# Own memory for the output projection's split activations, squares summed by VectorE, one tile for mean and deviation

## The chip, the cores and the metric

The kernel runs on one core of a Trainium2 chip. The metric is the device time of one execution in microseconds, the median over the runs shown. The profile is one further execution, recorded instruction by instruction.

## The reference

One layer of a hybrid encoder on 512 positions with 2048 channels. A combined projection feeds four groups of 1024 channels and a gate of 4096; each group's result is normalised, gated and projected back.

```python
h = rms_norm(x, pre_g)
proj = h @ w_in
a, f, hy, q, gate = split(proj, [2G, 3G, 6G, 7G])
# group 0, Conformer
u = a_val * sigmoid(a_gate)              # a_val, a_gate: the halves of a
u = depthwise_conv(u, conv_dw_w, conv_dw_b)
u = silu(layer_norm(u, conv_ln_g, conv_ln_b))
y_a = u @ conv_pw_w + conv_pw_b
# group 1: Fourier mixing of f; group 2: Hyena long convolution of hy;
# group 3: attention of q into 256 memory tokens
y = rms_norm(concat([y_a, y_b, y_c, y_m]) per group, group_g)
y = y * silu(gate)
out = y @ w_out
return x + rms_norm(out, post_g)
```

The layer norm subtracts the mean over 1024 channels, takes the mean of the squares of what is left, and scales. The norm of a group takes the mean of squares of its 1024 channels.

## The kernel before

Channels lie on the 128 partitions, positions along the free dimension: a group is CT = 8 tiles of 128 x 512. A product in full precision is made of three matmuls of a 32-bit format that TensorE takes in one pass (`mm3`, L102 to L105): each operand is split by `split` (L77) into a high part, copied by ScalarE (L79), and a rest, subtracted by VectorE (L80). Weights come through three buffers each of `raw`, `wh` and `wl`, 128 x 1024 (`load`, `wload`). TensorE's results go to PSUM: six banks with the tag `pg`, two with the tag `pf`.

`gate(g, ct, ...)` (L624) projects one gate tile in 48 matmuls into a `pf` bank (`project`, L304), takes its Silu on ScalarE and multiplies it into tile ct of group g; the group's scale `rsg[g]` (`group_scale`, L489) is multiplied in at the same place, or later by `group_norm` (L493) for the tiles gated before the norm was known. `project` calls its argument `fill` after every 12 matmuls, so that a generator's steps are laid between them. `channel_rstd` (L478) makes the deviation from a tile of summed squares: eight column sums on TensorE (L149), root on ScalarE and reciprocal on VectorE (L134, L135), a diagonal matrix by VectorE and its product with ones on TensorE (`spread`, L143, L144), and a copy to the tile asked for (L145).

The part in question comes after the attention (group 3, pool `wp3`). A pool `wp5` is opened with `lnt` (four tiles of 128 x 512: mean, deviation and two for squares), `uH` and `uL`. The eight tiles of the convolution lose their mean (L927); their squares are summed into `vacc` by `group_square` (L471): ScalarE squares into one of the two `lnt` tiles, GpSimd adds (L476). Then come `gate(3, 4)` and the last three gates of group 3, with the steps of `layer_norm` (L931) between their matmuls: `channel_rstd(rstd, vacc)` after 36 matmuls of `gate(3, 5)`, then one channel tile per step. The pointwise product (L948 to L961) follows in two halves of four `pg` banks; its results are squared and summed into `gacc` in the same way. `gA` takes the memory of `uL` for seven gate tiles that were computed early and are loaded back (L964). `gate(0, 7)` is the last projection. `group_norm(0)` scales one tile, and the loop at L970 scales seven and multiplies in `gA`: 15 VectorE instructions. Then `wp5` closes.

The output projection opens the pool `wp4` in the memory that `wp5` had. It goes through rounds of 512 output columns. In each, 32 tiles n of `y` are split into `jh` and `jl` (three buffers each, L1034 to L1036), in the order of the groups 2, 1, 3, 0; each n is 12 matmuls (four blocks of positions, three products). A pair of n shares one `wh`, `wl`. The last 512 columns are done in two rounds of two blocks each, six matmuls per n, and the results are finished (`finish`, L986) and stored.

The order on each engine is set by a planner when the program is built. It plays the program through on a clock of its own and gives each engine, among the instructions that are ready there, the earliest in the program. A tile waits for a free buffer of its tag; a pool's tiles wait until every pool that had their memory before has been read to the end. On the chip each engine goes through its list in order.

Of the kernel before, what the change touches and what calls it, by code (L numbers as in the profile page):

```python
# [12 lines left out]
F32R = mybir.dt.float32r  # L13
I32 = mybir.dt.int32
AF = mybir.ActivationFunctionType
# [5 lines left out]
P = 128  # L21
# [21 lines left out]
def encoder_kernel(ctx: ExitStack, tc: tile.TileContext, a: dict, out: bass.AP):  # L43
    nc = tc.nc
    act, dve, pool, pe, sp = nc.scalar, nc.vector, nc.gpsimd, nc.tensor, nc.sync
    mul, add, sub = ALU.mult, ALU.add, ALU.subtract
# [16 lines left out]
    def nm(s):  # L63
        uid[0] += 1
        return f"{s}_{uid[0]}"
# [4 lines left out]
    def pg():  # L70
        return psg.tile([P, 512], F32, tag="pg", name=nm("pg"))

    def ytile(i, dt=F32):
        return yp.tile([P, 4, 512], dt, tag=f"y{i}", name=nm(f"y{i}"))
# [10 lines left out]
    def load(src, n=1024):  # L85
        raw = stg.tile([P, 1024], F32, tag="raw", name=nm("raw"))
        sp.dma_start(raw[:, :n], src)
        return raw
# [4 lines left out]
    def wsplit(src, n=512):  # L93
        h, l = wparts()
        split(h[:, :n], l[:, :n], src)
        return h[:, :n], l[:, :n]

    def wload(src):

        return wsplit(load(src), 1024)  # L100

    def mm3(ps, wh, wl, xh, xl, start, stop):  # L102
        pe.matmul(ps, wh, xh, start=start, stop=False)  # L103
        pe.matmul(ps, wh, xl, start=False, stop=False)  # L104
        pe.matmul(ps, wl, xh, start=False, stop=stop)  # L105
# [49 lines left out]
    wp = w0.enter_context(tc.tile_pool(name="wx", bufs=2))  # L155

    def wt(tag, shape=(P, 512), dt=F32, bufs=2):
        return wp.tile(list(shape), dt, tag=tag, name=nm(tag), bufs=bufs)
# [213 lines left out]
    wp = w0.enter_context(tc.tile_pool(name="wpn", bufs=2))  # L372
# [7 lines left out]
    wp = w0.enter_context(tc.tile_pool(name="wp0", bufs=2))  # L380
# [90 lines left out]
    def group_square(src, acc, sqt, first):  # L471
        if first:
            act.activation(acc, src, AF.Square)
        else:
            act.activation(sqt, src, AF.Square)
            pool.tensor_tensor(acc, sqt, acc, op=add)  # L476
# [56 lines left out]
    wp = w1.enter_context(tc.tile_pool(name="wp1", bufs=2))  # L533
# [73 lines left out]
    gacc = cst.tile([P, 512], F32, tag="gacc", name="gaccC", bufs=2)  # L607
    for ct in range(CT):
# [5 lines left out]
        y = yC[ct // 4][:, ct % 4, :]  # L614
# [9 lines left out]
    def gate(g, ct, tiles, fill=None):  # L624
        ps = project(48 + CT * g + ct, fill)
        sg = sgtile()
        act.activation(sg, ps, AF.Silu)
        y = tiles[ct // 4][:, ct % 4, :]
        if g in rsg:
            group_scale(g, ct, tiles)  # L630
        else:
            gated.append((g, ct))
        dve.tensor_tensor(y, y, sg, op=mul)
# [3 lines left out]
    wp = w2.enter_context(tc.tile_pool(name="wp2", bufs=1))  # L637
# [6 lines left out]
    wp = w2i.enter_context(tc.tile_pool(name="wp2a", bufs=2))  # L644
# [8 lines left out]
    for k in range(KD):  # L653
# [8 lines left out]
        jh = wt("jh", (P, 514), F32R)  # L662
        jl = wt("jl", (P, 514), F32R)
# [30 lines left out]
    wp = w2i.enter_context(tc.tile_pool(name="wp2b", bufs=2))  # L694
# [70 lines left out]
    gacc = cst.tile([P, 512], F32, tag="gacc", name="gaccB", bufs=2)  # L765
# [50 lines left out]
    wp = w3.enter_context(tc.tile_pool(name="wp3", bufs=2))  # L816
    gacc = cst.tile([P, 512], F32, tag="gacc", name="gaccM", bufs=2)
# [93 lines left out]
    w3.close()  # L911


    w5 = ctx.enter_context(ExitStack())
    wp = w5.enter_context(tc.tile_pool(name="wp5", bufs=1))
    lnt = wt("lnt", (P, 4, 512), bufs=1)
    uH = wt("uH", (P, CT, 512), F32R, 1)
    uL = wt("uL", (P, CT, 512), F32R, 1)
    mean = lnt[:, 0, :]
    rstd = lnt[:, 1, :]  # L920
    pm = pg()
    pe.matmul(pm, ones, csum, start=True, stop=True)
    act.activation(mean, pm, AF.Copy, scale=1.0 / G)
    vacc = cst.tile([P, 512], F32, tag="gacc", name="vacc", bufs=2)
    for ct in range(CT):
        y = acch[ct // 4][:, ct % 4, :]
        dve.tensor_tensor(y, y, mean, op=sub)  # L927
        group_square(y, vacc, lnt[:, 2 + ct % 2, :], ct == 0)
    gate(3, 4, yM)

    def layer_norm():  # L931
# [15 lines left out]
    gacc = cst.tile([P, 512], F32, tag="gacc", name="gaccA", bufs=2)  # L947
    for hf in range(2):  # L948
        accs = [pg() for _ in range(4)]
        for kp in range(4):  # L950
            wh, wl = wload(a["pw"][hf, kp])
            for kk in range(2):
                k = 2 * kp + kk
                for m in range(4):
                    s = slice(512 * kk + P * m, 512 * kk + P * m + P)
                    mm3(accs[m], wh[:, s], wl[:, s], uH[:, k, :], uL[:, k, :], k == 0, k == CT - 1)
        for m in range(4):
            y = yA[hf][:, m, :]
            ct = 4 * hf + m
            act.activation(y, accs[m], AF.Identity, bias=pw_b[:, ct:ct + 1])  # L960
            group_square(y, gacc, lnt[:, 2 + ct % 2, :], ct == 0)  # L961
    gA = wt("uL", (P, CT, 512), F32, 1)
    for ct in range(EARLY):
        sp.dma_start(gA[:, ct, :], gdm[:, ct, :])  # L964
# [5 lines left out]
    for ct in range(EARLY):  # L970
        group_scale(0, ct, yA)
        y = yA[ct // 4][:, ct % 4, :]
# [6 lines left out]
    wp = w4.enter_context(tc.tile_pool(name="wp4", bufs=3))  # L979
# [6 lines left out]
    def finish(m):  # L986
        t = cst.tile([P, 1], F32, tag="st", name=nm("st"), bufs=2)
        dve.tensor_reduce(t, ssq[:, m, :], axis=AX.X, op=add)
        rst = rstd_of(t, 1, 1.0 / D)
        act.activation(og[:, m, 3, :], og[:, m, 3, :], AF.Copy, scale=rst)  # L990
        pool.tensor_tensor(xres[:, m, 3, :], xres[:, m, 3, :], og[:, m, 3, :], op=add)
        for r in range(3):
            dve.scalar_tensor_tensor(xres[:, m, r, :], og[:, m, r, :], rst, xres[:, m, r, :], op0=mul, op1=add)
            if r == 1:
                sp.dma_start(out[P * m:P * m + P, 0:1024], xres[:, m, 0:2, :].rearrange("p a b -> p (a b)"))
        for r in (2, 3):
            sp.dma_start(out[P * m:P * m + P, 512 * r:512 * r + 512], xres[:, m, r, :])
# [5 lines left out]
    for r, ms in rounds:  # L1003
        held = []
        accs = {m: (pg if r % 2 == 0 or m < 2 else pf)() for m in ms}
        gb = wt("gb", bufs=2)
        sp.dma_start(gb, a["post_g"][512 * r:512 * r + 512].partition_broadcast(P))
        c0, c1 = P * ms[0], P * ms[-1] + P
        for kp in range(16):
            if ms[0] == 2 and kp in (3, 6):  # L1010
                finish(kp // 3 - 1)
            i = 2 * kp - 32 + LAST
            if ms[0] == 2 and i >= 0:
                if i == 0:
                    lw = [ytile(0, F32R), ytile(1, F32R), ytile(4), ytile(5)]
                raw = lw[2 + i // 4][:, i % 4:i % 4 + 2, :].rearrange("p a b -> p (a b)")
                sp.dma_start(raw, a["wo"][r, order[2 * kp] // 2])
            else:
                raw = load(a["wo"][r, order[2 * kp] // 2])
            if not (ms[0] == 2 and i >= 0):  # L1020
                wh2, wl2 = wsplit(raw, 1024)
            for kk in range(2):
                k = order[2 * kp + kk]
                n = 2 * kp + kk
                if ms[0] == 2 and n >= 32 - LAST:
                    w = raw[:, 512 * kk:512 * kk + 512]
                    wh, wl = lw[(i + kk) // 4][:, (i + kk) % 4, :], wt("lwl", dt=F32R, bufs=LAST)
                    split(wh, wl, w)
                    jh, jl = (wt(t, (P, 256), F32R, LAST) for t in ("ljh", "ljl"))
                    split(jh, jl, ys[k // CT][k % CT // 4][:, k % 4, c0:c1])  # L1030
                    held.append((n, jh, jl, wh, wl))
                    continue
                wh, wl = wh2[:, 512 * kk:512 * kk + 512], wl2[:, 512 * kk:512 * kk + 512]
                jh = wt("jh", dt=F32R, bufs=3)  # L1034
                jl = wt("jl", dt=F32R, bufs=3)
                split(jh[:, c0:c1], jl[:, c0:c1], ys[k // CT][k % CT // 4][:, k % 4, c0:c1])  # L1036
                for m in ms:
                    s = slice(P * m, P * m + P)
                    mm3(accs[m], jh[:, s], jl[:, s], wh, wl, n == 0, n == 31)
        for m in ms:  # L1040
            for n, jh, jl, wh, wl in held:
                s = slice(P * m - c0, P * m - c0 + P)
                mm3(accs[m], jh[:, s], jl[:, s], wh, wl, False, n == 31)
            act.activation(og[:, m, r, :], accs[m], AF.Square, accum_out=ssq[:, m, r:r + 1])
            dve.tensor_tensor(og[:, m, r, :], accs[m], gb, op=mul)
            if ms[0] == 2:
                finish(m)
        if r == 2:
            act.activation(warm, ssq[:, 0, 2:3], AF.Sqrt)
# [119 lines left out]
```

## Time and profile before

| | us |
|---|---|
| runs (three) | 1730.17, 1731.67, 1737.29 |
| median | 1731.67 |
| the profiled execution | 1736.26 |
| its span in the profile | 1734.0 |

| engine | busy us | share of the span |
|---|---|---|
| TensorE (PE), matmuls | 1687.0 | 97% |
| TensorE, weight loads (PEld) | 1424.7 | 82% |
| VectorE (DVE) | 1205.5 | 70% |
| ScalarE (ACT) | 752.3 | 43% |
| GpSimd (POOL) | 151.4 | 9% |

Times in the rows are microseconds from the start of the span; the second number of a timeline row is how long the instructions of that row took together. A bracket at the end of a row is the engine's idle time before it and what ended that. Neighbouring matmuls overlap in the trace: a matmul's row says 0.39 us where the next starts after 0.23. PEclk is TensorE's granted clock as a share of its higher level.

### The profile page before, as it was taken

The numbers are of one execution on the slowest core, as the hardware profiler recorded it, in microseconds if no ns is written. First come the engines' busy times: TensorE is split into PE (matmuls) and PEld (weight loads), VectorE is DVE, ScalarE is ACT, GpSimd is POOL, SyncE is SP. The second block draws the span as 40 slices with busy tenths as digits, with TensorE's granted clock in tenths as the row PEclk, the third lists the DMA queues.
The fourth block names the chain that finished last, engine by engine and source line by source line (L and its number), as shares of the span: only waits on it lengthen the run. The fifth ranks groups of instructions, "written<-read, shape, count | busy, mean of one in ns | idle before, by whom it ended". The sixth has DMA issues, their size and how long they took to land.

```text
span 1734.0 us, 22272 instructions
## 1 busy us (share of the span) xinstructions
PE 1687.0 (97%) x8521; PEld 1424.7 (82%) x8521; DVE 1205.5 (70%) x1755; ACT 752.3 (43%) x1121; POOL 151.4 (9%) x98
## 2 busy tenths in 40 slices
PE   7999999999999999999999999999999699999997
PEld 5987888888888888888888898888878588888876
DVE  7966988478587686878765879986462545454586
ACT  6645655232223222223434346445453444444564
POOL 4201432000000000000000011100021100000000
PEclk9999999999999999999999999999999899999999
DMA  8654443432222322223333234232222523232355
GB/s 285 226 186 150 158 146 134 158 95 88 98 93 90 97 98 91 77 82 116 128 116 128 94 117 158 98 109 86 74 85 97 200 98 104 98 103 98 117 206 182
DMA packets 80575, 215.13 MB, mean 124 GB/s; under 512 B 8146, under 2 KB 25810, under 8 KB 79956
## 3 DMA queue, kind: packets, MB, share of 16 engines
q1 hardware_dynamic: 80468, 213.70, 36.5%
q8 instruction: 67, 1.10, 0.3%
q14 instruction: 40, 0.33, 0.1%
HBM read 195.05 MB, written 18.63 MB: 123 GB/s over the span
## 4 chain that ended last, share of the span: by engine, by line
PE 87%; DVE 7%; issue 2%; ACT 2%; DMA 2%; POOL 1%; SPq 0%; DVEq 0%; ACTq 0%; POOLq 0%
PE pf L105 16%; PE pf L103 16%; PE pf L104 16%; PE pg L103 12%; PE pg L104 12%; PE pg L105 12%; DVE y L516 2%; DVE wl L80 2%; DMA raw<-in_wv_dram 1%; POOL vacc L476 1%; ACT wh L79 1%; DMA kdm<-mst 0%; PE pg L558 0%; DVE y L491 0%; PE pg L411 0%
## 5 line engine op out<-in xcount | busy, mean ns | idle before, releaser
L103 PE MATMUL pf<-hH,wh 128*128 128x512 f32 x1280 | 504.7, 394 | 0.0
L105 PE MATMUL pf<-hH,wl 128*128 128x512 f32 x1280 | 502.1, 392 | 0.0
L104 PE MATMUL pf<-hL,wh 128*128 128x512 f32 x1280 | 501.5, 392 | 0.0
L80 DVE TENSOR_TENSOR wl<-raw,wh 128x1024 fp32r<-128x1024 f32 (+1 forms) x288 | 359.1, 1249 | 187.0 <-ACT wh L79 185.8
L79 ACT ACTIVATE wh<-raw 128x1024 fp32r<-128x1024 f32 (+1 forms) x288 | 298.3, 1037 | 358.9 <-PE pf L104 275.8
L103 PEld LDWEIGHTS pf<-hH,wh 128*128 128x128 f32 x1280 | 241.8, 189 | 47.7 <-issue 0.8
L105 PEld LDWEIGHTS pf<-hH,wl 128*128 128x128 f32 x1280 | 241.5, 189 | 47.4 <-issue 0.5
L104 PEld LDWEIGHTS pf<-hL,wh 128*128 128x128 f32 x1280 | 241.4, 189 | 47.2 <-issue 0.2
L80 DVE TENSOR_TENSOR jl<-y,jh 128x512 fp32r<-128x512 f32 (+1 forms) x154 | 91.5, 597 | 121.2 <-ACT jh L79 120.1
L79 ACT ACTIVATE jh<-y 128x512 fp32r<-128x512 f32 (+1 forms) x154 | 84.5, 550 | 179.3 <-PE pg L104 113.0
L103 PE MATMUL pg<-wh,jh 128*128 128x512 f32 x384 | 150.5, 392 | 11.2 <-ACT jh L79 11.2
L104 PE MATMUL pg<-wl,jh 128*128 128x512 f32 x384 | 150.2, 391 | 0.0
L105 PE MATMUL pg<-wh,jl 128*128 128x512 f32 x384 | 150.1, 391 | 0.0
L103 PEld LDWEIGHTS pg<-wh,jh 128*128 128x128 f32 x384 | 72.6, 189 | 26.4 <-ACT jh L79 11.5
L516 DVE SCALAR_TENSOR_TENSOR y<-ubuf,par,y 128x512 f32<-128x512 f32 x120 | 89.8, 748 | 2.5
L105 PEld LDWEIGHTS pg<-wh,jl 128*128 128x128 f32 x384 | 72.5, 189 | 15.4 <-DVE jl L80 0.2
L104 PEld LDWEIGHTS pg<-wl,jh 128*128 128x128 f32 x384 | 72.7, 189 | 15.1
L79 ACT ACTIVATE uH<-pp 128x512 fp32r<-128x512 f32 x16 | 10.1, 632 | 92.9 <-DVE pp L585 92.9
L516 DVE SCALAR_TENSOR_TENSOR y<-ub,par,y 128x512 f32<-128x512 f32 x60 | 46.4, 773 | 2.3 <-ACT y L514 1.1
L427 POOL TENSOR_TENSOR y<-fsq,y 128x512 f32<-128x512 f32 x24 | 43.6, 1815 | 41.5 <-ACT fsq L426 41.4
L104 PE MATMUL pf<-wl,jh 128*128 128x512 f32 x116 | 45.2, 390 | 1.3 <-DVE wl L80 1.3
L516 DVE SCALAR_TENSOR_TENSOR y<-ubm,par,y 128x512 f32<-128x512 f32 x60 | 45.2, 753 | 0.8
(374 smaller groups left out, 2847.3 us busy)
## 6 DMA issues: line engine op xcount, KB each, us to landing
raw<-in_w_std_dram SPq DMA_DIRECT2D x160, 512.0 KB, 3.8
raw<-in_wo_dram SPq DMA_DIRECT2D x77, 512.0 KB, 3.3
raw<-in_wk_dram SPq DMA_DIRECT2D x16, 512.0 KB, 4.0
kd<-y SPq DMA_DIRECT2D x16, 512.0 KB, 3.5
y<-kd SPq DMA_DIRECT2D x32, 256.0 KB, 3.3
raw<-in_w_f_dram SPq DMA_DIRECT2D x16, 512.0 KB, 3.3
raw<-in_wv_dram SPq DMA_DIRECT2D x15, 512.0 KB, 5.9
y<-in_xT_dram SPq DMA_DIRECT2D x8, 512.0 KB, 6.8
```

Source lines behind the costliest of these rows:

```text
L79: act.activation(h, src, AF.Copy)
L80: dve.tensor_tensor(l, src, h, op=sub)
L103: pe.matmul(ps, wh, xh, start=start, stop=False)
L104: pe.matmul(ps, wh, xl, start=False, stop=False)
L105: pe.matmul(ps, wl, xh, start=False, stop=stop)
L427: pool.tensor_tensor(acc, sq, acc, op=add)
L476: pool.tensor_tensor(acc, sqt, acc, op=add)
L516: dve.scalar_tensor_tensor(o, u[:, t:t + L], conv_w[:, ct, t:t + 1], o, op0=mul, op1=add)
```

## The change

It opens a small pool `wj` ahead of `wp5`, below it in memory, and keeps it open to the end. In round 0 all `jh` and `jl` come from `wj`, two buffers each; in later rounds two of three n take theirs from `wj` and the third from one buffer in `wp4`. `lnt` goes; one tile, `stat`, holds first the mean and then the deviation. The squares of the layer norm go to PSUM banks (`pg`) and are added by VectorE instead of GpSimd; those of group 0 go through the `stat` tile and are added by VectorE.

```diff
+    wj = ctx.enter_context(tc.tile_pool(name="wj", bufs=2))
     w5 = ctx.enter_context(ExitStack())
     wp = w5.enter_context(tc.tile_pool(name="wp5", bufs=1))
-    lnt = wt("lnt", (P, 4, 512), bufs=1)
     uH = wt("uH", (P, CT, 512), F32R, 1)
     uL = wt("uL", (P, CT, 512), F32R, 1)
-    mean = lnt[:, 0, :]
-    rstd = lnt[:, 1, :]
+    mean = rstd = wt("stat", bufs=1)
...
         dve.tensor_tensor(y, y, mean, op=sub)
-        group_square(y, vacc, lnt[:, 2 + ct % 2, :], ct == 0)
+        sq = vacc if ct == 0 else pg()
+        act.activation(sq, y, AF.Square)
+        if ct:
+            dve.tensor_tensor(vacc, sq, vacc, op=add)
...
             act.activation(y, accs[m], AF.Identity, bias=pw_b[:, ct:ct + 1])
-            group_square(y, gacc, lnt[:, 2 + ct % 2, :], ct == 0)
+            sq = gacc if ct == 0 else rstd
+            act.activation(sq, y, AF.Square)
+            if ct:
+                dve.tensor_tensor(gacc, sq, gacc, op=add)
...
-                jh = wt("jh", dt=F32R, bufs=3)
-                jl = wt("jl", dt=F32R, bufs=3)
+                jp, nb = (wj, 2) if r == 0 or n % 3 else (wp, 1)
+                jh, jl = (jp.tile([P, 512], F32R, tag=t, name=nm(t), bufs=nb) for t in ("jh", "jl"))
```

## Rows read from the trace of the kernel before

**Rows 1.** The page: busy time of each engine, share of the span, instructions.

```profile
PE 1687.0 (97%) x8521; PEld 1424.7 (82%) x8521; DVE 1205.5 (70%) x1755; ACT 752.3 (43%) x1121; POOL 151.4 (9%) x98
```

**Rows 2.** Stretches: length, busy PE, PEld, DVE, ACT, POOL; PEclk, DMA share, GB/s.

```profile
1251.50:1267.20 15.70, 15.70 (x71) 12.83 (x70) 13.20 (x15) 6.58 (x11) 10.14 (x5) 1.00 0.10 34
1267.20:1278.70 11.50, 7.99 (x29) 6.59 (x29) 6.46 (x10) 6.23 (x8) 3.05 (x3) 0.70 0.27 91
1300.60:1355.00 54.40, 54.40 (x242) 45.04 (x241) 13.99 (x11) 23.96 (x35) 10.82 (x7) 1.00 0.36 121
1355.00:1372.00 17.00, 2.93 (x18) 2.36 (x16) 12.77 (x23) 4.38 (x7) 0.00 (x0) 0.63 0.76 308
```

**Rows 3.** TensorE's timeline at the layer norm: start, duration, line, operands, idle before.

```profile
1251.47 0.47 PE L103 MATMUL pf<-hH,wh 128*128 128x512 f32 x1
...
1267.01 0.39 PE L105 MATMUL pf<-hH,wl 128*128 128x512 f32 x1
1270.91 1.87 PE L149 MATMUL pg<-ones,vacc 128*128 128x1 f32 x8 [3.51 <-POOL vacc L476]
```

**Rows 4.** TensorE's timeline at the entry of the output projection.

```profile
1354.99 0.95 PE L149 MATMUL pg<-ones,gaccA 128*128 128x1 f32 x8
...
1371.94 0.80 PE L103 MATMUL pg<-wh,jh 128*128 128x512 f32 x1 [11.19 <-ACT jh L79]
...
1376.89 0.40 PE L103 MATMUL pg<-wh,jh 128*128 128x512 f32 x1
```

**Rows 5.** The chain of work that ended last, in order of time: start, us, what.

```profile
1249.97 0.44 PE pg L144 x4
...
1274.27 0.43 PE pf L103
...
1361.42 2.08 DVE y L491 x3
...
1370.45 0.70 DVE y L973
```

**Rows 6.** Timelines of GpSimd and VectorE around both places.

```profile
1237.72 1.30 POOL L476 TENSOR_TENSOR gaccM<-sq,gaccM 128x512 f32<-128x512 f32 x1 [36.09 <-ACT sq L475]
1256.75 12.31 POOL L476 TENSOR_TENSOR vacc<-lnt,vacc 128x512 f32<-128x512 f32 x6 [15.70 <-ACT lnt L475]
...
1255.26 4.30 DVE L927 TENSOR_TENSOR y<-y,lnt 128x512 f32<-128x512 f32 x7
1259.48 1.78 DVE L491 SCALAR_TENSOR_TENSOR y<-y,par,rsg 128x512 f32<-128x512 f32 x1
1261.18 2.31 DVE L80 TENSOR_TENSOR wl<-raw,wh 128x1024 fp32r<-128x1024 f32 x1
...
1356.04 1.22 DVE L80 TENSOR_TENSOR wl<-raw,wh 128x1024 fp32r<-128x1024 f32 x1 [1.43 <-ACT wh L79]
```

**Rows 7.** ScalarE's and VectorE's groups from 1200 us on: busy us, mean ns, idle.

```profile
L79 ACT ACTIVATE wh<-raw 128x1024 fp32r<-128x1024 f32 x100 | 104.8, 1049 | 51.6 <-PE pf L104 26.1 <-PE pg L104 23.1 <-issue 1.8
L79 ACT ACTIVATE jh<-y 128x512 fp32r<-128x512 f32 x96 | 60.4, 631 | 154.8 <-PE pg L104 96.1 <-PE pf L104 48.8 <-DVE y L973 9.9
L1044 ACT ACTIVATE og<-pg 128x512 f32<-128x512 f32 x12 | 7.1, 595 | 1.5 <-PE pg L105 1.5
...
L80 DVE TENSOR_TENSOR wl<-raw,wh 128x1024 fp32r<-128x1024 f32 x100 | 124.6, 1246 | 88.2 <-ACT wh L79 88.0
L80 DVE TENSOR_TENSOR jl<-y,jh 128x512 fp32r<-128x512 f32 x96 | 66.4, 693 | 115.5 <-ACT jh L79 114.4 <-PE pg L104 1.1
L1045 DVE TENSOR_TENSOR og<-pg,gb 128x512 f32<-128x512 f32 x12 | 8.1, 689 | 1.4 <-ACT og L1044 1.3
```

**Rows 8.** TensorE's timeline in the last round.

```profile
1688.66 0.50 PE L104 MATMUL pf<-wl,jh 128*128 128x512 f32 x1 [1.28 <-DVE wl L80]
```

**Rows 9.** SP's queue of loads at the entry of the output projection.

```profile
1371.21 0.80 SPq L1007 DMA_DIRECT2D gb<-in_post_g_dram  x2
1382.47 11.21 SPq L87 DMA_DIRECT2D raw<-in_wo_dram  x3
```

## The prediction

> **What bounds the kernel now.** I read the page's busy times first: TensorE has 97% of the span [rows 1]. So a change is worth what it takes out of TensorE's gaps, and the table by stretches, from the last attention head on, tells where they are: 1267.2 to 1278.7 has TensorE at 7.99 of 11.50 us with a granted clock of 0.70, and 1355 to 1372 has it at 2.93 of 17.00 [rows 2]. TensorE's timeline names what it waits for there: 3.51 us for GpSimd's `vacc`, 11.19 us for ScalarE's `jh` [rows 3, 4]. The change touches these two places; call them A (layer norm) and B (entry of the output projection).
>
> **A, as it is.** The 69 matmuls from 1251.47 to 1267.01 come every 0.228 us [rows 3]: the last 33 of gate (3,4) and 36 of gate (3,5). Then TensorE idles, does its eight column sums in 1.87 us, where the same eight take 0.95 in B [rows 3, 4], and ten matmuls come every 0.43 us [rows 5]: behind the idle time the clock is at the lower of its levels (1.2 GHz), then back at 2.4. The work from 1267.24 to 1278.81, twelve matmuls further, is 0.95 + 2 x 0.44 (eight spread matmuls [rows 5]) + 12 x 0.228 = 4.6 us. The rest, 11.6 - 4.6 = **7.0 us**, is loss.
>
> **A, changed.** Removed: seven GpSimd adds, of which six stand in a chain of 12.31 us, 2.05 each; one with VectorE idle takes 1.30 [rows 6]. VectorE's work among them is stretched too: a scale of L491 takes 1.78 us (0.68 alone, as in the chain of B, three in 2.08 [rows 5]), a `wl` 2.31 (1.25) [rows 6, 7]. Added: seven VectorE adds of a PSUM and an SBUF operand. The nearest row is L1045, 0.689 us, as long as the SBUF pair of `jl`, 0.693 [rows 7]; seven subtractions in a row take 4.30, so 0.61 each [rows 6]. ScalarE's squares now write PSUM, which no row shows. A ScalarE copy within SBUF takes 0.631, a square out of PSUM 0.595 [rows 7]: 0.04 either way, 0.3 us for seven. I take zero, since they lie beside VectorE's work. (The Trainium skill, Trace Analysis, Optimizing Scalar/DVE Operations, gives VectorE some 65 ns more for an access to PSUM than to SBUF; by that seven adds would be 0.5 us longer, while the rows of L1045 and `jl` show no difference.)
>
> VectorE's queue decides what is left. Every engine goes in order, in an order fixed by the planner: of what its own clock has ready, the earliest in the program. From 1252.0 on VectorE has 8 subtractions and 7 adds at 0.61, five scales at 0.68, and then `wl` for the second half of gate (3,5) at 1.25: 9.2 + 3.4 + 1.25 = 13.8, done at 1265.8. TensorE wants it for that half's third matmul, 33 + 24 + 2 after 1251.47: 1264.9. So a stall of up to 0.9 us, none if a hole lets `wl` forward; I take 0.6. The sum in `vacc` is then ready near 1265, before TensorE comes to its place at 1267.2. A stall of 1.28 us elsewhere left the clock alone [rows 8]. **A gives 7.0 - 0.6 = 6.4 us**; bounds 2.6 (rival 4) and 7.0.
>
> **B, as it is.** Gate (0,7) ends, column sums to 1355.94, root on ScalarE, spread, then 15 multiplications of group 0 on VectorE from 1361.42 to 1371.15, then `jh`, then the first matmul of round 0 at 1371.94 [rows 4, 5]. That `jh` reads group 2, finished long before. It waits for memory: its pool opens only when all of `wp5`, `gA` with it, has been read, and the load of `gb`, which depends on no result, starts at 1371.21 as well [rows 9]. Round 0's first matmuls are at the low clock again; the 13th starts at 1376.89 [rows 4].
>
> **B, changed.** `wj` lies below `wp5`, where `wp3` was until about 1241. Two pairs `jh`, `jl` can be split in holes long before: ScalarE is busy 23.96 and VectorE 13.99 of 54.4 us from 1300.6 [rows 2]. Cost zero; 2 x (0.63 + 0.69) without holes. The weights of round 0's first three pairs of k are split by 1357.3 even now [rows 6]. So round 0 starts behind the column sums, at 1355.94, while the norm's chain goes on. 24 matmuls for two `jh` and the spread are 5.5 + 0.9, to 1362.3. The third `jh` gets its buffer after 12 matmuls, at 1358.7, and its `jl`, 0.63 + 0.69 later, comes before the multiplications. The fourth gets its buffer at 1362.3, and its `jl` is late: VectorE has begun the 15, which stand earlier in the program and block it to 1371.15. TensorE does n = 2 (to 1365.0) and the 8 of 12 matmuls of n = 3 that need no `jl` (to 1366.8), and idles 5.1 us until `jl` at 1371.9: long enough for the low clock, so ten more at 0.43, to 1376.4. At 1376.89 it has 44 + 10 + 2 = 56 matmuls behind it instead of 12: 44 x 0.228 = **10.0 us**. The planner's clock may shift one `jl` either way (rivals 1, 2).
>
> **The other pieces.** Adds of group 0's squares: seven at 0.69 on a VectorE that has 40 us of holes there. With one scratch tile each square waits for the add before it, and on ScalarE the next evictions and a `wh`, wanted two pairs later, stand behind: zero. Two buffers in round 0: `jh` and `jl` take 1.32 us [rows 7], TensorE has the other buffer for 12 x 0.228 = 2.7: zero. From round 1 on there are three again; at a round's border one of them comes 12 matmuls later (6 in round 3: 1.37 us): zero, up to 0.5. SP: `gb` waits as before, with the next weights behind it, which go at 1382.47 [rows 9]; they need the fourth `wl`, after 1371 in both kernels: zero. `mean` and `rstd` in one tile: the last reader of `mean` is done some 10 us before the write: zero.
>
> **Sum.** 6.4 + 10.0 = 16.4 us off the profiled execution: 1736.3 (span 1734.0 and 2.3 around it) to 1719.9. The median of the runs is 4.6 us lower; the same difference gives **1715.3 us**.
>
> **Rivals.** (1) `jl` of n = 2 falls behind the multiplications too: 32 x 0.228 = 7.3 in B, 1718.0; against it, 1.4 us of room. (2) The planner lets `jl` in between the multiplications, and round 0 runs through: its 13th matmul at 1355.94 + 0.9 + 2.7 = 1359.5 instead of 1376.89, 17.4 us in B, 1707.9; against it, 15 multiplications fill 1361.42 to 1371.15 without a hole [rows 5]. (3) The change doesn't do in B what it says: round 0 needs four of six PSUM banks beside two of the norm; if one is late, or the planner keeps the order, only A is left: 1725.3. (4) VectorE becomes the bound of A. It is busy 13.20 of 15.70 us there [rows 2]; with 7 x 0.69 more, 18.0: a stall of 2.3 us, and 2.1 us of low clock behind it, so A gives 2.6 and the time is 1719.1. Against it: some 4 of the 13.2 us are stretching beside GpSimd [rows 6]. The Trainium skill (Trace Analysis, Optimizing Scalar/DVE Operations) says that work of a saturated VectorE may go to ScalarE or even GpSimd, which speaks against this move. It adds that the two share a read port, so that this may not help, and the stretched rows agree with that. (5) **Slower:** two buffers starve round 0. If on each of its 15 pairs of k the two splits come behind `wh` and `wl` (1.05 and 1.25 us [rows 7]), 1.32 us become up to 3.6, over the 2.7 + 0.46 that TensorE has; a gap that drops the clock costs more than the harmless 1.28 and then 2.1 us, 3.4 each and 51 in all: 1766. From 5 such gaps on it loses everything. Against it: a `jh` is read for the last time before its `wh`, so its successor is ready first.
>
> **How the numbers follow.** Likeliest 0.46, rivals (1) 0.15, (2) 0.12, (3) 0.12, (4) 0.08, (5) 0.07. Half a percent (8.7 us) is about what a measurement of this kernel can tell from no change. Faster: 0.46 + 0.15 + 0.12 + 0.08 = 0.81; same: (3), 0.12; slower: (5), 0.07. The range, 1706 to 1726, takes in all but (5), with a microsecond or two at each end.
>
> **What would show it.** Right: no GpSimd add and no wait of TensorE at the sums of `vacc`, clock 1.00 there; round 0's first matmuls right behind the sums of `gaccA`; then one gap of some 5 us, ended by a `jl` behind the last of the 15 multiplications. Wrong: a wait for `wl` of over 1 us in gate (3,5); round 0 starting after 1370; gaps every 24 matmuls in round 0.

## The result and the profile after

The changed kernel takes 1716.22 us (median of four runs, 1714.06 to 1719.62) where the kernel before takes 1733.12 on the same chip: a ratio of 0.990, with a 95% interval of 0.9882 to 0.9918, so 17.3 us (14.2 to 20.5). Measured a second time it gave 1716.43 us and 0.9895 (0.9878 to 0.9911). The forecast was 1715.3.

The page of the kernel after, its busy times (before: [rows 1]):

```profile
PE 1681.8 (98%) x8521; PEld 1421.9 (83%) x8521; DVE 1211.1 (71%) x1769; ACT 752.5 (44%) x1121; POOL 128.3 (7%) x84
```

GpSimd has 14 instructions fewer and VectorE 14 more: seven adds of the layer norm and seven of group 0. TensorE is busy 5.2 us less with the same 8521 matmuls, which fits fewer of them at the low clock.

The waits of TensorE from 1240 us on, where the change touches its work: what waited, for what, us in total, times, longest. First the kernel before, then the one after:

```profile
PE pg L103 <- ACT jh L79: 11.2, 1, 11.2
PE pg L149 <- POOL vacc L476: 3.5, 1, 3.5
PE pg L144 <- DVE diag L143: 2.9, 2, 2.7
...
```

```profile
PE pg L144 <- DVE diag L143: 2.8, 1, 2.8
PE pg L105 <- DVE jl L80: 1.8, 1, 1.8
PE pf L104 <- DVE wl L80: 1.2, 1, 1.2
```

The waits for `vacc` and for `jh` are gone. Instead there is one of 1.8 us for a `jl`. The one for the spread (L144) was there before, but its price was hidden: the long wait for `jh` followed it. The table by stretches of the kernel after (length; busy PE, PEld, DVE, ACT, POOL; PEclk, DMA share, GB/s; before: [rows 2]):

```profile
1249.00:1264.60 15.60, 15.60 (x77) 13.09 (x76) 14.87 (x24) 11.94 (x16) 0.00 (x0) 1.00 0.00 1
1264.60:1276.00 11.40, 11.40 (x56) 9.53 (x55) 10.78 (x19) 6.80 (x11) 0.00 (x0) 1.00 0.51 169
1345.80:1349.50 3.70, 0.93 (x10) 0.85 (x8) 2.67 (x6) 3.07 (x5) 0.00 (x0) 0.81 0.63 230
1349.50:1355.00 5.50, 5.50 (x17) 4.79 (x18) 3.04 (x7) 0.60 (x1) 0.00 (x0) 0.51 0.99 416
1355.00:1360.30 5.30, 5.30 (x24) 4.16 (x23) 5.30 (x9) 2.22 (x3) 0.00 (x0) 1.00 0.95 397
1360.30:1363.40 3.10, 1.26 (x6) 0.89 (x6) 3.10 (x6) 1.04 (x2) 0.00 (x0) 1.00 0.00 0
```

In A (the first two rows) TensorE is busy without a hole and the clock is 1.00 throughout. VectorE, at 14.87 of 15.60 us, is nearly full, and yet TensorE does not wait for it. In B (the other four) the clock is still low from 1349.5 to 1355, behind the wait for the spread; behind the wait for `jl` it is not.

**Where the 18.9 us between the two profiled executions (spans 1734.0 and 1715.1) went.** Three marks of TensorE's timeline cut the trace: the column sums of `gaccM` ahead of gate (3,4), the first matmul of the pointwise convolution, and the column sums of `gaccA`. The kernel before, then the kernel after (the last mark of before is in [rows 4]):

```profile
1245.49 0.95 PE L149 MATMUL pg<-ones,gaccM 128*128 128x1 f32 x8
...
1300.58 0.39 PE L103 MATMUL pg<-uH,wh 128*128 128x512 f32 x1
```

```profile
1243.28 0.95 PE L149 MATMUL pg<-ones,gaccM 128*128 128x1 f32 x8
...
1291.36 0.39 PE L103 MATMUL pg<-uH,wh 128*128 128x512 f32 x1
...
1345.77 0.95 PE L149 MATMUL pg<-ones,gaccA 128*128 128x1 f32 x8
```

From the first to the second is A: 55.09 us before, 48.08 after, **7.0 us** less. From the second to the third is the pointwise convolution, where squares of group 0 are now added by VectorE: 54.41 in both. From the third to the span's end is B with the output projection: 379.0 before, 369.3 after, **9.7 us** less (10.3 in the second profile). The other 2.2 us lie ahead of the first mark, where the change adds nothing but the first two splits of `jh` and `jl`, beside TensorE's work. Over the nine profiles of changed kernels shown below this mark lies anywhere from 1242.58 to 1245.53, and in two of the same kernel at 1243.28 and 1244.58. It is scatter of an execution, and it belongs to no step.

### The profile page after: what moved, and what is told of

The parts are those of the page before. It is cut to its first block, busy times and chain, and to the rows that moved or that the text cites. A ratio compares the mean times of both kernels' runs of the same rounds, so it can differ in the third digit from the quotient of the medians.

```text
span 1715.1 us, 22245 instructions
## 1 busy us (share of the span) xinstructions
PE 1681.8 (98%) x8521; PEld 1421.9 (83%) x8521; DVE 1211.1 (71%) x1769; ACT 752.5 (44%) x1121; POOL 128.3 (7%) x84
## 4 chain that ended last, share of the span: by engine, by line
PE 87%; DVE 7%; DMA 2%; ACT 2%; issue 2%; SPq 0%; DVEq 0%; ACTq 0%
PE pf L105 17%; PE pf L103 17%; PE pf L104 17%; PE pg L103 12%; PE pg L104 12%; PE pg L105 12%; DVE wl L80 2%; DVE y L516 2%; DMA raw<-in_wv_dram 1%; ACT wh L79 1%; PE pg L558 0%; DMA kdm<-mst 0%; PE pg L411 0%; DMA uL<-gdm 0%; PE pg L412 0%
## 5 line engine op out<-in xcount | busy, mean ns | idle before, releaser
L105 PE MATMUL pf<-hH,wl 128*128 128x512 f32 x1280 | 501.6, 392 | 0.0
L105 PEld LDWEIGHTS pf<-hH,wl 128*128 128x128 f32 x1280 | 241.3, 188 | 47.1 <-issue 0.5
L105 PE MATMUL pg<-wh,jl 128*128 128x512 f32 x384 | 149.7, 391 | 1.8 <-DVE jl L80 1.8
L105 PEld LDWEIGHTS pg<-wh,jl 128*128 128x128 f32 x384 | 72.5, 189 | 17.4 <-DVE jl L80 2.3
```

## The experiments

The three stretches of every kernel, in us, each read from the same three marks of its own timeline and its span. A is from the sums of `gaccM` to the pointwise convolution, PW the convolution, B from the sums of `gaccA` to the end. Gains are against the profile of the kernel before; each ratio is against its runs on the same chip, whose median was 1733.1, 1733.9 and 1734.8 us in the three sets.

| kernel | A | PW | B to the end | gain A + B | median | ratio (95%) |
|---|---|---|---|---|---|---|
| before | 55.09 | 54.41 | 379.0 | | 1733.1 to 1734.8 | |
| after | 48.08 | 54.41 | 369.3 | 7.0 + 9.7 | 1716.2 | 0.990 (0.9882 to 0.9918) |
| after_again | 48.10 | 54.41 | 368.7 | 7.0 + 10.3 | 1716.4 | 0.9895 (0.9878 to 0.9911) |
| a_alone | 48.08 | 54.41 | 379.0 | 7.0 + 0.0 | 1728.9 | 0.9965 (0.9952 to 0.9978) |
| a_sbuf | 48.65 | 54.41 | 379.3 | 6.4 - 0.3 | 1728.0 | 0.9965 (0.9952 to 0.9978) |
| b_alone | 54.92 | 54.40 | 368.8 | 0.2 + 10.2 | 1723.8 | 0.9944 (0.9925 to 0.9963) |
| norm_pf | 48.09 | 54.40 | 368.6 | 7.0 + 10.4 | 1715.8 | 0.9893 (0.9879 to 0.9908) |
| defer | 48.10 | 54.40 | 367.7 | 7.0 + 11.3 | 1714.6 | 0.9888 (0.9874 to 0.9903) |
| defer_pf | 48.09 | 54.41 | 361.7 | 7.0 + 17.3 | 1709.1 | 0.9856 (0.984 to 0.9872) |
| one_buf | 48.08 | 54.41 | 397.6 | 7.0 - 18.6 | 1745.7 | 1.0067 (1.0052 to 1.0082) |

**a_alone: the layer norm's part without the output projection's.** Of the change, `wj` is left out:

```diff
-    wj = ctx.enter_context(tc.tile_pool(name="wj", bufs=2))
...
-                jp, nb = (wj, 2) if r == 0 or n % 3 else (wp, 1)
-                jh, jl = (jp.tile([P, 512], F32R, tag=t, name=nm(t), bufs=nb) for t in ("jh", "jl"))
+                jh = wt("jh", dt=F32R, bufs=3)
+                jl = wt("jl", dt=F32R, bufs=3)
```

> The layer norm's part alone: squares into PSUM banks and the shared tile for mean and deviation are kept, the output projection takes its jh and jl from wp4 again, three buffers each, as in the kernel before. If the two parts are independent, this one is worth the 7.0 us that the traces of before and after show from gate (3,4)'s first matmul to the first matmul of the pointwise convolution (54.27 and 47.27): 7.0 us under the kernel before (0.4%), and TensorE waits some 11 us for jh at the entry of round 0, with the low clock behind it, as before. Rival: VectorE's extra adds also cost something in the pointwise convolution, or the shared tile does, and the change hides it behind B: then the gain is under 5 us. Rival 2: part of B's gain comes from the earlier end of A (other holes): then the gap for jh is clearly under 11 us.

Measured: 0.9965, 6.1 us (3.8 to 8.3). The stretches say it more closely: A gives 7.0, PW nothing, B nothing. Its waits from 1240 us on:

```profile
PE pg L103 <- ACT jh L79: 11.2, 1, 11.2
...
```

The wait for `jh` is as long as before although A ends 7 us earlier, so nothing of B's gain comes from A, and both rivals fall. It also fits the prediction's reading of that wait: memory set it, and not the time at which something was ready.

**b_alone: the output projection's part without the layer norm's.** `wj` and the shared tile are kept, but GpSimd adds all squares again, with its scratch in the buffers of `wj` that nobody has yet:

```diff
-        sq = vacc if ct == 0 else pg()
-        act.activation(sq, y, AF.Square)
-        if ct:
-            dve.tensor_tensor(vacc, sq, vacc, op=add)
+        group_square(y, vacc, None if ct == 0 else wj.tile([P, 512], F32, tag="jl", name=nm("sqj"), bufs=2), ct == 0)
...
+            group_square(y, gacc, None if ct == 0 else wj.tile([P, 512], F32, tag="jl", name=nm("sqj"), bufs=2), ct == 0)
```

> The own memory of jh and jl alone: GpSimd adds the squares again, both in the layer norm and in group 0, with the square's scratch tile in the buffers of wj that are not yet in use. Expected 9.8 us under the kernel before (0.6%), the gain measured between the traces from the end of the column sums of gaccA to the 37th matmul of round 0 (26.41 to 16.65 us); at the layer norm the wait of TensorE for vacc of some 3.5 us and the granted clock of 0.51 behind it are back. Rival: GpSimd's adds in group 0 lie beside VectorE's splits and round 0's first jh and jl come later, or the two parts help each other: then under 8 us or over 11. A rival for A: the wait at the layer norm came from the scratch tile lnt and not from GpSimd's adds: then TensorE does not wait for vacc here.

Measured: 0.9944, 9.7 us (6.4 to 13.0); A 0.2, B 10.2. Its waits:

```profile
PE pg L149 <- POOL vacc L476: 3.5, 1, 3.5
PE pg L144 <- DVE diag L143: 2.7, 1, 2.7
PE pg L105 <- DVE jl L80: 2.4, 1, 2.4
...
```

The wait for `vacc` is back, with `lnt` gone: it was GpSimd's adds, not the tile that held the scratch. The wait for `jh` is not back, and B gives all it gives in the change. The two parts are independent, 7.0 and some 10, and add up.

**a_sbuf: does PSUM cost anything?** As a_alone, with two SBUF tiles for the squares in place of PSUM banks:

```diff
+    lsq = wt("lsq", (P, 2, 512), bufs=1)
...
-        sq = vacc if ct == 0 else pg()
+        sq = vacc if ct == 0 else lsq[:, ct % 2, :]
```

> The layer norm's part alone, as in the kernel a_alone, but the squares go through two SBUF tiles and not through PSUM banks; VectorE adds them as in a_alone. It tells the price of PSUM as the place of the squares. Theory: none; the whole gain of 7.0 us comes from the adds' move off GpSimd: from the column sums of gaccM to the first matmul of the pointwise convolution 48.08 us as in a_alone and the changed kernel, seven adds at 0.69 each in both, squares within 0.05 us of each other. Rival: an operand in PSUM costs VectorE some 65 ns an add: adds of 0.62 to 0.63 here, and a stall that was not there with them can not go, so the time is the same. Rival 2: the squares in SBUF make ScalarE and VectorE collide: the stretch is longer by over 0.5 us.

The groups of adds and squares from 1240 to 1275 us (mean ns behind the busy time), a_alone and then a_sbuf:

```profile
L931 DVE TENSOR_TENSOR vacc<-pg,vacc 128x512 f32<-128x512 f32 x7 | 4.8, 682 | 0.0
L929 ACT ACTIVATE pg<-y 128x512 f32<-128x512 f32 x7 | 4.1, 597 | 2.0 <-DVE y L927 2.0
```

```profile
L932 DVE TENSOR_TENSOR vacc<-lsq,vacc 128x512 f32<-128x512 f32 x7 | 4.8, 682 | 0.0
L930 ACT ACTIVATE lsq<-y 128x512 f32<-128x512 f32 x7 | 4.3, 629 | 2.5 <-DVE y L928 1.3 <-DVE vacc L932 1.1
```

An add takes 682 ns from either place, so the first rival falls; a square is 32 ns shorter into PSUM. (The Trainium skill, Perfetto Trace Analysis, Optimizing Scalar/DVE Operations, gives VectorE some 65 ns more for an access to PSUM and ScalarE some 42 ns less; the second agrees with these rows in sign and roughly in size, the first does not.) A is 48.65 us here, 0.57 longer, and the last line tells one reason: with two tiles, 1.1 us of ScalarE's waits are for VectorE's add to free one. The last add comes later, and with it the column sums. The second rival is thus right in size, by just over its 0.5 us, but not in its cause: VectorE's adds are as long as with PSUM, and ScalarE's seven squares 0.2 us longer in all. So 6.4 of A's 7.0 us come with the adds' move off GpSimd, and the banks, six of them against two tiles, are worth the last half a microsecond. The theory had the whole 7.0 for the move.

**norm_pf: why round 0 waited for the spread.** The prediction had round 0 start right behind the column sums of `gaccA`. TensorE's timeline of the kernel after shows otherwise (start, duration, line, operands, idle before; the column sums are the last mark above):

```profile
1349.49 1.22 PE L144 MATMUL pg<-diag,ones 128*128 128x128 f32 x4 [2.77 <-DVE diag L143]
1350.36 0.77 PE L103 MATMUL pg<-wh,jh 128*128 128x512 f32 x1
...
1360.09 0.39 PE L104 MATMUL pg<-wl,jh 128*128 128x512 f32 x1
1362.32 1.21 PE L105 MATMUL pg<-wh,jl 128*128 128x512 f32 x4 [1.84 <-DVE jl L80]
1363.37 0.40 PE L103 MATMUL pg<-wh,jh 128*128 128x512 f32 x1
```

Round 0's first matmul is at 1350.36, behind the first half of the spread, with its `jh` and `jl` split near 1240 us. Theory T1: its four banks carry the tag `pg`, as the spread does, and banks of one tag are handed out in the program's order. The edit gives the norm another tag:

```diff
-    group_norm(0, gacc, yA)
+    group_norm(0, gacc, yA, pf)
```

> The changed kernel, with the two PSUM results of group 0's norm (column sums and spread) taken from the tag pf instead of pg. Theory T1: banks of one tag are handed out in the order of the program, so round 0's four banks wait until the spread, which stands ahead of them, has taken its own; with another tag for the norm, round 0's first matmul follows the column sums at once: no idle time of 2.77 us there and no low clock at its start. Then jl of n = 2 comes before the 15 multiplications, 44 matmuls are done before TensorE waits for jl of n = 3, that wait is some 5 us and the clock falls behind it, as the prediction had it: 10.7 us in B against 9.8, so 0.9 us under the changed kernel, with 2.7 either way. Rival T2: something else holds round 0 back (its weights, the planner's clock): the order at the entry and the 2.77 us stay as they are, and the time too.

```profile
1345.12 0.95 PE L149 MATMUL pf<-ones,gaccA 128*128 128x1 f32 x8
1345.94 0.48 PE L103 MATMUL pg<-wh,jh 128*128 128x512 f32 x1
...
1349.44 0.61 PE L144 MATMUL pf<-diag,ones 128*128 128x128 f32 x4
...
1356.70 0.39 PE L104 MATMUL pg<-wl,jh 128*128 128x512 f32 x1
1361.51 2.08 PE L105 MATMUL pg<-wh,jl 128*128 128x512 f32 x4 [4.42 <-DVE jl L80]
1363.38 0.63 PE L103 MATMUL pg<-wh,jh 128*128 128x512 f32 x1
```

T2 falls, and the start that T1 foretold comes: with the norm on another tag round 0 starts 0.82 us behind the start of the sums. So the shared tag held it back. That it does so by the order in which banks are handed out stays an argument. The edit also leaves `pg` two banks more; that six are enough, four for round 0 and two for the norm, is a count and no run. This is the prediction's picture, step by step: 44 matmuls before the gap, one gap of 4.42 us (5.1 forecast), and the low clock behind it (four in 2.08 us, then 0.43 each). And it is worth next to nothing: B is 0.1 to 0.7 us shorter than in the two profiles of the kernel after (0.9 expected). In both kernels the wait ends with a `jl` that comes near the end of the 15 multiplications, 16.5 us behind the start of the sums in the kernel after and 16.3 here. With 44 instead of 32 matmuls done by then, 12 x 0.228 = 2.7 us are gained. But 11 matmuls at 0.43 instead of 0.228 follow, 2.2 us. The kernel after has its low clock ahead of that wait, where slow matmuls only make the wait shorter.

**defer and defer_pf: the block of multiplications.** VectorE's timeline of the kernel after shows what the `jl` stood behind:

```profile
1352.66 2.08 DVE L491 SCALAR_TENSOR_TENSOR y<-y,par,rsg 128x512 f32<-128x512 f32 x3 [1.62 <-ACT rsg L145]
...
1360.91 0.75 DVE L491 SCALAR_TENSOR_TENSOR y<-y,par,rsg 128x512 f32<-128x512 f32 x1
1361.58 0.69 DVE L80 TENSOR_TENSOR jl<-y,jh 128x512 fp32r<-128x512 f32 x1
1362.18 0.69 DVE L980 TENSOR_TENSOR y<-y,uL 128x512 f32<-128x512 f32 x1
```

Fourteen of the 15 multiplications stand ahead of it, one behind the other from 1352.66 on. The edit leaves the one of `group_norm` where it is and puts the loop's 14 into round 0, two at a time, from the fourth pair of k on; the group's `y` are wanted only in the last quarter of a round. The pool `wp4` and the load of `gb` follow them:

```diff
-    for ct in range(EARLY):
+    def scale_rest(ct):
...
+            if r == 0 and 3 <= kp < 3 + EARLY:
+                scale_rest(kp - 3)
+            elif r == 0 and kp == 3 + EARLY:
+                w5.close()
+                w4 = ctx.enter_context(ExitStack())
```

> The changed kernel with the 15 multiplications of group 0 put two by two into pairs 3 to 9 of round 0, and nothing else (the norm's PSUM results stay in the tag pg). Cause to be told apart: the block of multiplications ahead of the third jl. If the wait of 1.84 us for jl of n = 2 is due to that block alone, it goes and nothing else changes: the wait of 2.77 us for the spread and the low clock behind it stay as they are, and the 37th matmul of round 0 comes some 14.8 us behind the end of the column sums instead of 16.65. 1.9 us under the changed kernel, 0.1%; more exactly the length of round 0 tells it. Rival: what the two gaps cost is not independent (a shift of the queue, the clock): then it differs from the 17.3 of the kernel with both edits less the price of the first gap, 17.3 - 5.6 = 11.7 us in B.

> The changed kernel, with the norm's banks of the tag pf as in norm_pf, and the 15 multiplications of group 0 put two by two into the first half of round 0 (pairs 3 to 9 of k) instead of ahead of it; the pool wp4 and the load of gb follow at pair 10. If the two causes are the bank's order (T1) and the block of multiplications ahead of jl, TensorE has no gap of over 1 us from the column sums of gaccA on: its 37th matmul of round 0 comes 0.9 + 36 x 0.228 = 9.1 us behind the sums' end instead of 16.65: 7.6 us under the changed kernel, 24.5 under the kernel before. Rival: T2, the gap of 2.77 us and the low clock stay, and only the 1.84 us go: 2.2 us under the changed kernel. Rival 2: the multiplications spread over round 0 delay splits of weights there, and gaps of over 1 us come further on: same as the changed kernel or slower.

The waits of TensorE from 1240 us on, defer and then defer_pf:

```profile
PE pg L144 <- DVE diag L143: 2.7, 1, 2.7
PE pf L104 <- DVE wl L80: 1.2, 1, 1.2
...
```

```profile
PE pf L104 <- DVE wl L80: 1.2, 1, 1.2
```

With the block away the wait for that `jl` goes, and the one for the spread stays (a new one of 0.3 us, for another `jl`, comes in the last round): B gains 11.3 us, where 11.7 was expected, 1.0 to 1.7 over the kernel after. By the medians of one chip (1714.6 and 1716.4) this can't be told from no change; the trace tells it. With both edits neither wait is left, B gains 17.3, as expected (9.7 + 7.6), and the 37th matmul of round 0 comes 9.99 us behind the start of the sums. That kernel is faster than both: 0.9856 of the one before. The first wait with its low clock, taken away when the second is gone already, is worth 17.3 - 11.3 = 6.0 us; taken away alone (norm_pf), 0.1 to 0.7.

**one_buf: what the buffers are worth.** Two buffers in round 0 are one fewer than before, and the prediction costed that at nothing. A third in round 0 was not tried; this kernel takes one more away:

```diff
-    wj = ctx.enter_context(tc.tile_pool(name="wj", bufs=2))
+    wj = ctx.enter_context(tc.tile_pool(name="wj", bufs=1))
...
-                jp, nb = (wj, 2) if r == 0 or n % 3 else (wp, 1)
+                jp, nb = (wj, 1) if r == 0 or n % 3 == 0 else (wp, 2)
```

> The changed kernel with one buffer each for jh and jl in round 0 instead of two (from round 1 on the three are dealt out 1 in wj and 2 in wp4). It prices the buffers that the change takes from round 0, by taking one more. Theory: two are enough since a split takes 1.32 us and TensorE has 2.7 us of the other buffer; with one, each n waits for the split of jh behind the last matmul that read the one before: some 0.63 + 0.2 us idle, some 30 times, at full clock since each gap is under 1.28 us: about 25 us slower than the changed kernel (20 to 43), 1741. Rival: TensorE's order among the twelve matmuls hides even that: same. Rival 2, the prediction's slower case: gaps that come again and again drop the clock as well, 2 us or more each: 60 to 100 us slower.

Its waits, two neighbouring ones in TensorE's timeline, and the clock of a stretch of four:

```profile
PE pg L103 <- ACT jh L79: 16.3, 31, 1.4
PE pg L105 <- DVE jl L80: 3.6, 1, 3.6
```

```profile
1389.81 0.50 PE L103 MATMUL pg<-wh,jh 128*128 128x512 f32 x1 [0.49 <-ACT jh L79]
...
1393.32 0.50 PE L103 MATMUL pg<-wh,jh 128*128 128x512 f32 x1 [0.49 <-ACT jh L79]
```

```profile
1386.30:1400.30 14.00, 12.05 (x48) 8.70 (x48) 5.20 (x6) 4.39 (x7) 0.00 (x0) 1.00 0.23 76
```

Slower by 29.3 us than the kernel after (25 expected, 20 to 43). Every n now takes 3.51 us instead of 12 x 0.228 = 2.73, at the full clock: over the four n of that stretch it is 1.00. So the theory holds and both rivals fall. The 31 n make 31 x 0.78 = 24 us of it; at the entry the wait for `jl` is 3.6 us long instead of 1.8 to 2.1, and the clock is low behind it (four matmuls in 2.07 us, then 0.43 each). With two buffers no wait of TensorE for `jh` is in the list of the kernel after: the second buffer hides the split whole. At the entry a third might still have been worth something: the `jl` that TensorE waits for there belongs to the third n, whose `jh` starts only at 1355.73, when the first n has given its buffer back and the block of multiplications has begun. No run shows that.

**after_again: the changed kernel once more**, unedited, to measure the scatter.

> The changed kernel itself, beside the others on the same chip, as the measure for differences of one or two us between them: 0.990 of the kernel before, as the first time (0.9882 to 0.9918); its layer norm 48.08 us from the column sums of gaccM to the first matmul of the pointwise convolution, and its 37th matmul of round 0 16.65 us behind the end of the column sums of gaccA. If these two do not come out again within 0.1 us, what was read from one profile of it is scatter.

A came out again to 0.02 us. B did not: the 37th matmul of round 0 is 17.02 us behind the start of the column sums instead of 17.60 (16.65 behind their end), 0.6 less, where 0.1 was expected. The rows of the second profile tell why:

```profile
1350.76 0.71 PE L144 MATMUL pg<-diag,ones 128*128 128x128 f32 x4 [2.72 <-DVE diag L143]
1351.22 0.47 PE L103 MATMUL pg<-wh,jh 128*128 128x512 f32 x1
1351.62 1.12 PE L144 MATMUL pg<-diag,ones 128*128 128x128 f32 x4
```

Behind the same wait the first four spread matmuls take 0.71 us here and 1.22 in the first profile: the clock falls a little later, the spread is done 0.6 us earlier (5.65 us behind the start of the sums instead of 6.21), and with it the multiplications and the `jl`. So differences of B under 0.6 us, norm_pf against the kernel after among them, are within scatter.

## Why the prediction was right, step by step

The forecast was 16.4 us of gain, 6.4 in A and 10.0 in B. Measured were 7.0 and 9.7 (10.3 the second time). The sum is right, and A's mechanism too. B came to its number by another route, and in part by luck.

**A, what the adds cost.** Right: GpSimd's adds off the path, no wait at the sums, clock 1.00, no price for PSUM, none for the squares on ScalarE. The rows of the adds say 0.68 to 0.69 us, but neighbouring ones overlap, and VectorE starts one every 0.60, as the forecast took it (0.61).

**A, the stall for `wl`.** The step that was mis-sized, by 0.6 us. The forecast had `wl` of gate (3,5)'s second half done some 0.9 us after TensorE's need, and took 0.6 as lost. VectorE was as late as that:

```profile
1262.65 1.22 DVE L80 TENSOR_TENSOR wl<-raw,wh 128x1024 fp32r<-128x1024 f32 x1
```

But TensorE did not stand still meanwhile:

```profile
1262.76 0.39 PE L103 MATMUL pf<-hH,wh 128*128 128x512 f32 x1
...
1263.22 0.95 PE L149 MATMUL pg<-ones,vacc 128*128 128x1 f32 x8
1264.03 0.48 PE L105 MATMUL pf<-hH,wl 128*128 128x512 f32 x1
```

Where the first matmul with `wl` (L105) would have waited, the planner put a further pair without `wl` and the eight column sums, which the earlier adds had made ready. I had the sums at their old place, behind the gate. In a_sbuf, where the sums are ready later, they can't fill that hole.

**B, the start of round 0.** Wrong: "round 0 starts behind the column sums". I counted banks, and they were free; that they are handed out within one tag in the program's order I had not asked. norm_pf shows that the tag decides it. The order of handing out is the explanation that I take for it; the runs show only the tag's part.

**B, what follows.** The step from that start to "44 matmuls" and "5.1 us" fell with it. It was 32 matmuls, a wait of 2.77 with the low clock behind it, and one of 1.84 without. But rightly foreseen was what ends the last wait, a `jl` behind VectorE's block of multiplications, and that sets when both routes go on; norm_pf, which takes the forecast's route, gains 10.4. The rival (1), the third `jl` behind the block, is what happened in its order of work. Its price was too low: 7.3 us for 32 matmuls, with a low clock behind the gap as before. There was none behind 1.84 us, which is worth 2.1 (rival 4's figure for it), and the `jl` came ahead of the last multiplication and not behind it, 0.6: 7.3 + 2.1 + 0.6 = 10.0. That this is the forecast's number is luck: 12 matmuls fewer, 2.7 us, against 2.1 + 0.6 that the forecast did not have.

**The other pieces.** Zero each, as forecast: PW 54.41 us in both, no wait of TensorE for a buffer past the entry, and nothing behind the entry but the wait of 1.2 us in the last round, which was there before [rows 8].

**The rivals.** (2) had `jl` between the multiplications, and 17.4 us in B. The planner did let it in, but only ahead of the last of 15. Its price was right: defer_pf, which runs through, gains 17.3. (3) fell, with a grain of truth: the planner kept the order for the spread alone. (4) fell by 14.87 of 15.60 us, no more room than 0.7. (5) fell: one_buf shows that starving takes one buffer fewer, and costs 0.8 us per n and not 3.4 per pair, as the clock stayed at 1.00 behind those waits.

## What to carry to other kernels

Where several waits stand between the same two events, the one that ends last sets the time: take an earlier one away and the later one grows by nearly as much (norm_pf gains 0.1 to 0.7 us), take the last one away first and the other is worth its full price (6.0). A program's order can hide in resources too: here work that was ready stood behind a tile of the same tag that was not, and another tag let it past (norm_pf). Before work is moved onto an engine that looks full, look at its queue for who else is waiting there, and at the other engines' lists for what could fill the hole.

## What the runs showed of the hardware that was not expected

From 1240 us on TensorE's clock fell to the lower of its two levels behind waits of 2.72, 2.77, 3.52, 3.6 and 4.42 us, and stayed at the higher behind waits of 1.84, 2.1 and 2.4, and behind 31 waits of some 0.5. That is no rule by the length of one wait. Near 185 us, far from the change, TensorE does the same work ahead of a wait of 1.47 us in the kernel before and in the kernel after (the wait, then the stretch behind it):

```profile
187.33 0.47 PE L411 MATMUL pg<-fwH,h2s 128*128 128x512 f32 x1 [1.47 <-DVE y L447]
187.40:190.00 2.60, 2.60 (x12) 2.15 (x13) 2.60 (x5) 0.63 (x1) 0.00 (x0) 1.00 0.96 321
```

```profile
183.87 0.56 PE L411 MATMUL pg<-fwH,h2s 128*128 128x512 f32 x1 [1.47 <-DVE y L447]
183.90:186.50 2.60, 2.60 (x7) 2.05 (x8) 2.60 (x5) 0.63 (x1) 0.00 (x0) 0.54 0.90 276
```

The clock is 1.00 behind the one and 0.54 behind the other. Of the nine profiles with this wait at 1.47 or 1.48 us it fell in seven. So that it stayed high behind the 1.84 us of the kernel after need not come out in every execution.

After equal waits of 2.72 us for the spread it fell at different moments: ahead of the first four spread matmuls in defer (1.22 us), as after the 2.77 of the kernel after, behind them in after_again (0.71), and behind all eight in one_buf (0.71 twice). Between the two profiles of the kernel after that is the 0.6 us in B. The wait of 2.7 us for the spread stands in the waits of the kernel before already. I had expected round 0 to fill it, so I had not asked what it would cost if it stayed.
